# Splitting the second mixer's weights into DRAM during the first MLP

## The chip, the cores and the metric

The kernel runs on one core of a Trainium2 chip. The metric is device time in microseconds, the median of several runs. A core has five engines that matter here: TensorE (PE) for matmuls, VectorE (DVE) and ScalarE (ACT) for everything by element, GpSimd (POOL, almost unused) and SyncE (SP), which only issues DMAs. Each engine executes its own instructions in order. ACT can issue DMAs too.

## The reference

A trunk of two layers, 512 tokens with 16 meta tokens put ahead of them (528 positions), width 1024, fp32. Each layer is a mixer and an MLP, each between two RMS norms:

```
a = rmsnorm(h, mix_pre_g[l])
proj = a @ w_in[l]                      # q, k, v, b_gate, c_gate, hc
y_attn = sliding_window_gqa_sinks(q, k, v, sinks[l])   # q, k with partial rope
y_conv = short_gated_conv(b_gate, c_gate, hc, conv_w[l])
y = concatenate([rmsnorm(y_attn, attn_out_g[l]), rmsnorm(y_conv, conv_out_g[l])])
h = h + rmsnorm(y @ w_out[l], mix_post_g[l])
a = rmsnorm(h, mlp_pre_g[l])
f = square(relu(a @ w_up[l])) @ w_down[l]
h = h + rmsnorm(f, mlp_post_g[l])
```

`w_in` is 1024 x 2304, `w_out` 1024 x 1024, `w_up` 1024 x 4096, `w_down` 4096 x 1024, for each layer.

## The kernel before

Everything is kept transposed: channels on the 128 partitions, 8 blocks of them, and the 528 positions along the free axis. For accuracy each fp32 operand is split into a high part, rounded to the matmul's fp32r format, and a low part, the rest. A product of one block is three matmuls (`mm3`, L196 to L198): high by high, high by low, low by high.

Weights come in tiles of 1024 x 128. The list `blocks` names them in the order of use: for each mixer 2 tiles for k and v, 4 for q, 12 for the convolution's three inputs ("in") and 8 of the output projection ("out"); then the MLP in four chunks of 1024 hidden channels. Chunk 0 has 8 plain "up" tiles and 8 "down" tiles. Chunks 1 to 3 have 28 units of "upx" each, which are the seven products of Strassen's scheme for four pairs of tiles (`fast_pair`), and then 8 down tiles.

`prep()` (L134) makes a tile ready. SP loads its two halves of 256 KB each to `wraw` (5 buffers), and `cast()` splits each half: ACT copies it to the high part (L107), and DVE subtracts that from the raw half, which gives the low part (L108). High and low parts lie in 14 slots "w". After each tile used, `tile_done()` and `refill()` prepare further ones, so that up to 14 units are ready or under way. For two layers that is 264 splits of plain halves, and others for the pairs.

`mlp()` runs the chunks. `one()` multiplies one tile with both ranges of positions (A and B; in layer 0 two products of 24 matmuls) and evacuates each product from its PSUM bank: an up tile by `f_evac` (DVE's max, ACT's square, then a split into f_hi and f_lo), a down tile by `z_evac` (ACT copies for chunk 0, DVE adds for the others). In chunk 3 `one()` runs the first two down tiles only; the other six go to `boundary()`, where the last products in range B overlap with the norm of the first range and the next mixer's first products. There `Post` makes the norm's factor s (`chain`, L248 and L249), then for each block of channels the product with z (L326), the new h (L327), and a_hi and a_lo. `first_tiles` multiplies the mixer's k, v and first q tiles. After k and q are evacuated, the rope exchanges rows by small DMAs on SP (L558, L559), which stand in SP's order among the loads of weights.

The order of each engine's instructions is set by a scheduler, which simulates the program in time and places each instruction where it expects it to be ready. So an instruction written at one place can stand later on its engine, and from then on the order is fixed. All DMAs of weights are issued by SP in the kernel before; ACT issues a few at the start and two at the end.

Of the kernel before, what the change touches and what calls it, by code (L numbers as in the profile page):

```python
# [8 lines left out]
F32 = mybir.dt.float32  # L9
F32R = mybir.dt.float32r  # L10
AF = mybir.ActivationFunctionType
ALU = mybir.AluOpType

P = 128
# [22 lines left out]
def trunk_kernel(ctx, tc, xT, gains, sinkb, sinkm, rope, masks, maskm, ident_in, w_in, w_out, w_up, w_down, outT):  # L37
    nc = tc.nc
    ACT, DVE, POOL, PE = nc.scalar, nc.vector, nc.gpsimd, nc.tensor
# [3 lines left out]
    cp = ctx.enter_context(tc.tile_pool(name="cp", bufs=1))  # L43
# [7 lines left out]
    def tmp(w=272):  # L51
        return tp.tile([P, 272], F32, tag="t", name="t", bufs=8)[:, :w]
# [24 lines left out]

    epst = cp.tile([P, 4], F32, name="epst")

    blocks = []  # L80
    for l in range(2):
        blocks += [("in", l, 512), ("in", l, 640)]
# [13 lines left out]
    prepared = []  # L96
    last_load = []
# [5 lines left out]
    def half():  # L103
        return wp.tile([P, 4, P], F32, tag="wraw", name="wraw", bufs=5)

    def cast(raw, hi, lo):
        ACT.activation(hi, raw, AF.Copy)  # L107
        DVE.tensor_tensor(lo, raw, hi.bitcast(F32), ALU.subtract)  # L108
# [4 lines left out]
    def prep_pair(l, m, n):  # L113
# [17 lines left out]
        cast(pair[("A11", "S2", "S3", "S1", "A12", "A22", "S4")[n]], f[:, 0:4, :], f[:, 4:8, :])  # L131
        prepared.append((f[:, 0:4, :], f[:, 4:8, :]))

    def prep(beside=None):  # L134

        if len(prepared) == len(blocks):
            return
        taken[0] += size(len(prepared))
        kind, l, sub = blocks[len(prepared)]
        if kind == "upx":  # L140
            return prep_pair(l, *sub)
        hi = wp.tile([P, KT, P], F32R, tag="w", name="whi", bufs=2 * CAP)
        lo = wp.tile([P, KT, P], F32R, tag="w", name="wlo", bufs=2 * CAP)
        raws = []
        for i in range(2):
            raw = half()
            raws.append(raw)
            ks = slice(4 * i, 4 * i + 4)
            dma = nc.sync.dma_start
            if kind == "out":  # L150
                col = slice(P * sub, P * sub + P)
                if i == 0:
                    for g in range(2):
                        dma(raw[g * 64:(g + 1) * 64], w_out[l, g * 256:(g + 1) * 256, col].rearrange("(j p) m -> p j m", p=64))
                else:
                    dma(raw, w_out[l, 512:1024, col].rearrange("(k p) m -> p k m", p=P))
            elif kind == "q":
                for g in range(2):
                    last_load[:] = [dma(raw[:, :, 64 * g:64 * g + 64], w_in[l].rearrange("(k p) m -> p k m", p=P)[
                        :, ks, 256 * g + 64 * sub:256 * g + 64 * sub + 64])]  # L160
            elif kind == "down":
                c, m = sub
                dma(raw, w_down[l, c * 1024:(c + 1) * 1024, P * m:P * m + P].rearrange("(k p) m -> p k m", p=P)[:, ks, :])
            else:
                src, off = (w_in, sub) if kind == "in" else (w_up, P * sub)
                last_load[:] = [dma(raw, src[l].rearrange("(k p) m -> p k m", p=P)[:, ks, off:off + P])]
            if beside:

                beside[2 * i]()
                cast(raw, hi[:, ks, :], lo[:, ks, :])  # L170
                beside[2 * i + 1]()
        if not beside:
            for i in range(2):
                ks = slice(4 * i, 4 * i + 4)
                cast(raws[i], hi[:, ks, :], lo[:, ks, :])
        prepared.append((hi, lo))
# [8 lines left out]
    def refill(most=9):  # L185
        while len(prepared) < len(blocks) and taken[0] + size(len(prepared)) <= 2 * cap[0] and most:
            prep()
            most -= 1

    def tile_done(most=9):  # L190
        taken[0] -= size(done[0])
        done[0] += 1
        refill(most)
# [23 lines left out]
    def gemm(item, act):  # L217
        for ev in mms([item], act):
            ev()
# [31 lines left out]
    def utile():  # L251
        return tp.tile([P, L + 2], F32, tag="u", name="u", bufs=2)
# [2 lines left out]
        return tp.tile([P, 272], F32, tag="s", name="s", bufs=2)[:, :n]  # L255

    pend = []

    def flush():
        while pend:  # L260
            pend.pop(0)()
# [239 lines left out]
    def z_evac(m, r, add, final, col):  # L501

        t0, t1 = r
        l, c = col
        g = gt[:, l, c + m:c + m + 1]

        def ev(ps):
            zz = z[:, m, t0:t1]
            if add:
                DVE.tensor_tensor(zz, zz, ps, ALU.add)  # L510
                if final and l == 1 and m == 7 and r == RB:
                    sq = tmp(t1 - t0)
                    ACT.activation(sq, zz, AF.Square)
                    last_sq.append(sq)
                elif final:
                    add_sq("z", m == 0, zz, r)
                if final:
                    if l == 1:
                        ACT.activation(zz, zz, AF.Copy, scale=g)
            elif final:  # L520
                ACT.activation(zz, ps, AF.Copy, scale=g)
                add_sq("z", m == 0, ps, r)
            else:
                ACT.activation(zz, ps, AF.Copy)
        return ev

    class Mixer:
# [367 lines left out]
    def f_evac(m, r):  # L895
        t0, t1 = r

        def ev(ps):
            f = tmp(t1 - t0) if t1 - t0 <= 272 else utile()[:, :t1 - t0]
            DVE.tensor_scalar(f, ps, 0.0, None, ALU.max)  # L900
            ACT.activation(f, f, AF.Square)
            split(f_hi[:, m, t0:t1], f_lo[:, m, t0:t1], f)
        return ev

# [79 lines left out]
    def mlp(l, nxt, first):  # L984

        xr = xrange(l)

        full = xr if l == 0 else [(xr[0][0], xr[1][1])]

        def one(evac, act):  # L990
            w = wtile()
            for r in full:
                gemm((w, r, evac(r)), act)
            tile_done()

        txs[l] = [wp.tile([P, 4, L // 2], F32R, tag="x", name="tx", bufs=3) for _ in range(3)]
        for c in range(NCH):
            if c == 0:
                for m in range(NA, 8):
                    one(lambda r: f_evac(m, r), act_a)  # L1000
            else:
                for m in range(0, 8, 2):
                    fast_pair(l, m)
            last = c == NCH - 1
            if last:
                new_acc("h")
            for m in range(2 if last else 8):
                one(lambda r: z_evac(m, r, c > 0, last, (l, G_MPOST)), act_f)
                if c == 0 and m < 4:
                    fast_sums(l, m)  # L1010
        if nxt is not None:
            clear_pad()
        w = wtiles(6)
        for m in range(6):
            gemm((w[m], xr[0], z_evac(2 + m, xr[0], True, True, (l, G_MPOST))), act_f)
        boundary(l, w, act_f, G_MPOST, lambda r: Post(l, G_MPOST, r, nxt), first)
# [87 lines left out]
```

## Time and profile before

| | |
|---|---|
| median of 3 runs | 1096.59 us (1096.15 to 1097.74) |
| profiled execution | 1097.51 us |
| span in its profile | 1095.7 us |
| TensorE busy | 1074.3 us, 98% |
| DVE busy | 801.3 us, 73% |
| ACT busy | 624.6 us, 57% |
| DMA | mean 93 GB/s, 102.06 MB |

The first mixer ends and the first MLP's products begin near 180 to 230 us; chunk 0's down tiles run until 295 us, then pairs and down tiles alternate until 562 us; the second mixer runs until about 700 us, the second MLP to the end. In rows of groups of instructions the columns are: line, engine, operation, what is written from what, count, then busy time and mean duration, then idle time just ahead of them and what ended most of it.

### The profile page before, as it was taken

Reading aid. Unit: us, or ns where it says so; the run is one execution under the profiler, and the core shown is the slowest. Engines: PE = TensorE matmul, PEld = TensorE weight load, DVE = VectorE, ACT = ScalarE, POOL = GpSimd, SP = SyncE. Lnnn points to the kernel's source line nnn. Section 1 sums busy time; section 2 is a strip of 40 time slices with the busy share of each in tenths; the row PEclk is TensorE's granted clock in tenths of the full one; section 3 lists DMA queues with packets and bytes.
Section 4 is the critical chain, followed back from the end, with each engine's and each line's share of the span. In section 5 each row is a group of like instructions: output and inputs, shape, how many; then the busy total and the mean of one; then the engine's idle time right before and its main releaser. Section 6 shows DMA issues by size and latency. Waiting matters only on the chain.

```text
span 1095.7 us, 21642 instructions
## 1 busy us (share of the span) xinstructions
PE 1074.3 (98%) x8196; PEld 1030.8 (94%) x8196; DVE 801.3 (73%) x1895; ACT 624.6 (57%) x1510; POOL 10.8 (1%) x44
## 2 busy tenths in 40 slices
PE   8999999999999999999999999999999999999995
PEld 8999999999999999999989999999889989989995
DVE  7797886977585586586597988779947757757735
ACT  7576766665472383275365676667636625725732
POOL 2000000000000000000000000000000000000000
PEclk9999999999999999999999999999999999999998
DMA  9252122252252243144141412232422522522402
GB/s 249 64 146 59 58 78 79 77 155 59 69 152 85 59 127 110 49 124 137 26 112 39 130 58 59 78 97 82 130 72 84 154 68 79 162 68 71 143 1 77
DMA packets 206057, 102.06 MB, mean 93 GB/s; under 512 B 24000, under 2 KB 205904, under 8 KB 205952
## 3 DMA queue, kind: packets, MB, share of 16 engines
q1 hardware_dynamic: 205088, 99.89, 31.9%
q8 instruction: 64, 1.05, 0.4%
q10 hardware_dynamic: 688, 0.58, 0.2%
q14 instruction: 41, 0.34, 0.1%
q0 software_dynamic: 176, 0.21, 0.1%
HBM read 97.88 MB, written 2.10 MB: 91 GB/s over the span
## 4 chain that ended last, share of the span: by engine, by line
PE 88%; DVE 7%; ACT 1%; DMA 1%; issue 1%; SPq 1%; DVEq 0%; ACTq 0%
PE ps L196 28%; PE ps L198 28%; PE ps L197 28%; PE ps L202 1%; PE ps L684 1%; PE ps L653 1%; DVE wlo L108 1%; DVE a_lo L338 1%; DVE h L327 1%; DVE acc L280 1%; PE ps L235 1%; DMA h<-in_xT 0%; DVE t L326 0%; DMA z<-t 0%; SPq L558 0%
## 5 line engine op out<-in xcount | busy, mean ns | idle before, releaser
L197 PE MATMUL ps<-f_lo,whi 128*128 128x256 f32 (+2 forms) x1072 | 326.1, 305 | 0.0
L198 PE MATMUL ps<-f_hi,wlo 128*128 128x256 f32 (+2 forms) x1072 | 325.5, 305 | 0.0
L196 PE MATMUL ps<-f_hi,whi 128*128 128x256 f32 (+2 forms) x1072 | 322.9, 306 | 0.0
L197 PE MATMUL ps<-a_lo,whi 128*128 128x256 f32 (+3 forms) x808 | 230.2, 289 | 2.0 <-DVE a_lo L338 1.7
L196 PE MATMUL ps<-a_hi,whi 128*128 128x256 f32 (+3 forms) x808 | 227.2, 294 | 4.8 <-ACT a_hi L380 1.9
L198 PE MATMUL ps<-a_hi,wlo 128*128 128x256 f32 (+3 forms) x808 | 229.2, 288 | 0.1
L108 DVE TENSOR_TENSOR wlo<-wraw,whi 128x512 fp32r<-128x512 f32 x264 | 174.2, 688 | 51.8 <-ACT whi L107 31.5
L198 PEld LDWEIGHTS ps<-f_hi,wlo 128*128 128x128 f32 x1072 | 202.1, 189 | 9.1
L197 PEld LDWEIGHTS ps<-f_lo,whi 128*128 128x128 f32 x1072 | 201.6, 188 | 9.5
L107 ACT ACTIVATE whi<-wraw 128x512 fp32r<-128x512 f32 x264 | 153.9, 624 | 95.4 <-PE ps L197 58.4
L196 PEld LDWEIGHTS ps<-f_hi,whi 128*128 128x128 f32 x1072 | 199.5, 188 | 9.4
L196 PEld LDWEIGHTS ps<-a_hi,whi 128*128 128x128 f32 x808 | 148.1, 189 | 9.9 <-ACT a_hi L380 2.3
L197 PEld LDWEIGHTS ps<-a_lo,whi 128*128 128x128 f32 x808 | 152.6, 189 | 5.0 <-DVE a_lo L338 2.6
L198 PEld LDWEIGHTS ps<-a_hi,wlo 128*128 128x128 f32 x808 | 152.9, 189 | 1.4 <-DVE wlo L108 0.3
L510 DVE TENSOR_TENSOR z<-z,ps 128x272 f32<-128x272 f32 (+2 forms) x78 | 38.0, 487 | 99.9 <-PE ps L198 99.8
L107 ACT ACTIVATE wf<-wraw 128x512 fp32r<-128x512 f32 x96 | 59.7, 626 | 85.4 <-PE ps L197 51.8
L197 PE MATMUL ps<-a_lo,wf 128*128 128x264 f32 (+1 forms) x384 | 108.0, 282 | 0.0
L196 PE MATMUL ps<-a_hi,wf 128*128 128x264 f32 (+1 forms) x384 | 107.8, 282 | 0.0
L198 PE MATMUL ps<-a_hi,wf 128*128 128x264 f32 (+1 forms) x384 | 107.1, 283 | 0.0
L107 ACT ACTIVATE wf<-u 128x512 fp32r<-128x512 f32 x72 | 45.1, 627 | 88.4 <-PE ps L197 73.6
L108 DVE TENSOR_TENSOR wf<-wraw,wf 128x512 fp32r<-128x512 f32 x96 | 65.7, 688 | 11.5 <-ACT wf L107 10.5
L197 PEld LDWEIGHTS ps<-a_lo,wf 128*128 128x128 f32 x384 | 72.2, 188 | 0.1
(158 smaller groups left out, 1776.5 us busy)
## 6 DMA issues: line engine op xcount, KB each, us to landing
wraw<-in_w_up SPq DMA_DIRECT2D x128, 256.0 KB
wraw<-in_w_down SPq DMA_DIRECT2D x128, 256.0 KB
wraw<-in_w_in SPq DMA_DIRECT2D x56, 256.0 KB
wraw<-in_w_in SPq DMA_DIRECT2D x32, 128.0 KB
wraw<-in_w_out SPq DMA_DIRECT2D x32, 128.0 KB
wraw<-in_w_out SPq DMA_DIRECT2D x16, 256.0 KB
h<-in_xT SPq DMA_DIRECT2D x4, 272.0 KB
h<-in_xT SPq DMA_DIRECT2D x4, 256.0 KB
```

The lines of the kernel that those rows point to most:

```text
L107: ACT.activation(hi, raw, AF.Copy)
L108: DVE.tensor_tensor(lo, raw, hi.bitcast(F32), ALU.subtract)
L196: PE.matmul(ps, whi, ahi, start=first, stop=False, skip_group_check=onto)
L197: PE.matmul(ps, whi, alo, start=False, stop=False, skip_group_check=onto)
L198: PE.matmul(ps, wlo, ahi, start=False, stop=last, skip_group_check=onto)
L202: PE.matmul(ps, a[n], b[n], start=first and n == 0, stop=last and n == 1)
L235: PE.matmul(ps, ones[:, which, :], acc, start=True, stop=more is None)
L280: return (eng or DVE).tensor_tensor(acc, acc, sq, ALU.add)
L327: DVE.tensor_tensor(hk, hk, t, ALU.add)
L338: DVE.scalar_tensor_tensor(a_lo[:, k, t0:t1], hk, g, a_hi[:, k, t0:t1].bitcast(F32), ALU.mult, ALU.subtract)
L510: DVE.tensor_tensor(zz, zz, ps, ALU.add)
L653: PE.matmul(outs[g], q[a][rows], k[b][rows], start=n == 0, stop=n == 2)
```

## The change

Two buffers are added in SBUF: `sr` for a raw half of a tile, `sf` for its high and low parts. A new function `stash()` is called behind each product of `one()` in layer 0, and its instructions are queued behind that product's evacuation (`issue_after`). Each call takes one half of one of the second mixer's 26 tiles: it splits the half in `sr` into `sf` (ACT and DVE), ACT issues a store of `sf` (512 KB) to a tile in DRAM, and ACT issues the load of the next half into `sr`. The first call only loads. There are 58 calls and 52 halves, so the last calls do nothing. When `prep()` comes to such a tile, SP loads its four pieces (256 KB each) from DRAM straight into two slots "w", and nothing is split there. The matmuls are the same. The lines of `prep()` that loaded a half are moved to `load_half()`, for both uses.

```
+    sr = cp.tile([P, 4, P], F32, name="sr")
+    sf = cp.tile([P, 2, 4, P], F32R, name="sf")
+    dp = ctx.enter_context(tc.tile_pool(name="dp", bufs=1, space=bass.MemoryType.DRAM))
...
+    def load_half(queue, raw, kind, l, sub, i):
+        ks = slice(4 * i, 4 * i + 4)
+        dma = queue.dma_start
+        if kind == "out":
+            col = slice(P * sub, P * sub + P)
+            if i == 0:
+                for g in range(2):
+                    dma(raw[g * 64:(g + 1) * 64], w_out[l, g * 256:(g + 1) * 256, col].rearrange("(j p) m -> p j m", p=64))
+            else:
+                dma(raw, w_out[l, 512:1024, col].rearrange("(k p) m -> p k m", p=P))
+        elif kind == "q":
+            for g in range(2):
+                last_load[:] = [dma(raw[:, :, 64 * g:64 * g + 64], w_in[l].rearrange("(k p) m -> p k m", p=P)[
+                    :, ks, 256 * g + 64 * sub:256 * g + 64 * sub + 64])]
...
+    stashed = {}
+    to_stash = [(b, i) for b in blocks if b[1] == 1 and b[0] in ("in", "q", "out") for i in range(2)]
+
+    def stash():
+
+        if not to_stash:
+            return
+        if not stashed:
+            stashed[None] = None
+            return stash_load()
+        (kind, l, sub), i = to_stash.pop(0)
+        cast(sr, sf[:, 0], sf[:, 1])
+        t = dp.tile([P, 2, 4, P], F32R, name=f"st_{kind}_{sub}_{i}")
+        ACT.dma_start(t.bitcast(F32), sf.bitcast(F32))
+        stashed.setdefault((kind, l, sub), []).append(t)
+        stash_load()
+
+    def stash_load():
+        if to_stash:
+            block, i = to_stash[0]
+            load_half(ACT, sr, *block, i)
...
+        if (kind, l, sub) in stashed:
+            src = stashed[(kind, l, sub)]
+            for n, t in enumerate((hi, lo)):
+                for i in range(2):
+                    nc.sync.dma_start(t[:, 4 * i:4 * i + 4, :].bitcast(F32), src[i][:, n].bitcast(F32))
+            prepared.append((hi, lo))
+            return
...
+                last_ev[:] = [DVE.tensor_tensor(zz, zz, ps, ALU.add)]
...
+                last_ev[:] = [ACT.activation(zz, ps, AF.Copy)]
...
+            last_ev[:] = [ACT.activation(f, f, AF.Square)]
...
                 gemm((w, r, evac(r)), act)
+                if l == 0:
+                    with tc.issue_after(last_ev[0].ins):
+                        stash()
```

Lines shift by the added ones: the cast's two instructions are L113 and L114 in the changed kernel, the stash's store L174, its loads of "in" L159, the reloads L197.

DVE where the stash begins, in chunk 0 of the first MLP, in the changed kernel (wlo, wraw and whi belong to the usual splits, f_lo to an up tile):

```order
L940 TENSOR_SCALAR t_3433<-ps_3408 128x256
L114 TENSOR_TENSOR wlo_3444<-wraw_3445,whi_3443 128x512
L114 TENSOR_TENSOR wlo_3444<-wraw_3447,whi_3443 128x512
L114 TENSOR_TENSOR sf_88<-sr_87,sf_88 128x512
L324 TENSOR_TENSOR f_lo_73<-t_3433,f_hi_72 128x256
```

The first step's subtraction stands behind the two of a weight tile that were there before.

DVE at the layer boundary before (s is the norm's factor, L326 and L327 are the first steps of Post):

```order
L108 TENSOR_TENSOR wlo_7585<-wraw_7586,whi_7584 128x512
L108 TENSOR_TENSOR wlo_7585<-wraw_7588,whi_7584 128x512
L248 SCALAR_TENSOR_TENSOR t_7647<-ps_7643,t_7647 128x256
L249 SCALAR_TENSOR_TENSOR s_7642<-t_7647,t_7646 128x256
L326 SCALAR_TENSOR_TENSOR t_7680<-z_69,gt_76,s_7642 128x256
L326 SCALAR_TENSOR_TENSOR t_7685<-z_69,gt_76,s_7642 128x256
L327 TENSOR_TENSOR h_68<-h_68,t_7680 128x256
```

and at the same place now:

```order
L320 TENSOR_TENSOR acc_7247<-acc_7247,t_7792 128x272
L320 TENSOR_TENSOR acc_3080<-acc_3080,t_7829 128x256
L287 SCALAR_TENSOR_TENSOR t_7891<-ps_7887,t_7891 128x256
L288 SCALAR_TENSOR_TENSOR s_7886<-t_7891,t_7890 128x256
L114 TENSOR_TENSOR sf_88<-sr_87,sf_88 128x512
L366 SCALAR_TENSOR_TENSOR t_7924<-z_69,gt_76,s_7886 128x256
L366 SCALAR_TENSOR_TENSOR t_7929<-z_69,gt_76,s_7886 128x256
```

The two splits ahead of the norm are gone, and the subtraction of the 52nd step stands between s and the first product of Post.

ACT in the pairs of chunk 1, in the changed kernel (wf are the pairs' split weights, t and f_hi belong to the evacuation of products):

```order
L113 ACTIVATE wf_4522<-wraw_4443 128x512
L113 ACTIVATE sf_88<-sr_87 128x512
L997 ACTIVATE t_4504<-t_4504 128x264
L113 ACTIVATE wf_4542<-wraw_4441 128x512
L1013 ACTIVATE t_4525<-t_4525 128x264
L998 ACTIVATE t_4504<-t_4504 128x264
L323 ACTIVATE f_hi_72<-t_4525 128x264
L323 ACTIVATE f_hi_72<-t_4504 128x264
L113 ACTIVATE wf_4563<-u_4464 128x512
L174 DMA st_q_3_1_3924<-sf_88 128x1024
L159 DMA sr_87<-in_w_in 128x4x128
L997 ACTIVATE t_4545<-t_4545 128x264
```

Three instructions of a step, the cast, the store and the next load, now stand among those that evacuate the pairs' products, though no call of `stash()` is written there.

SP among the rope's exchanges of the second mixer, before:

```order
L558 DMA z_69<-t_7845 8x256
L559 DMA z_69<-t_7845 8x256
L166 DMA wraw_8075<-in_w_in 128x4x128
L166 DMA wraw_8164<-in_w_in 128x4x128
L166 DMA wraw_8166<-in_w_in 128x4x128
L558 DMA z_69<-t_7957 8x256
L559 DMA z_69<-t_7957 8x256
```

and in the changed kernel:

```order
L599 DMA z_69<-t_8246 8x256
L197 DMA whi_8264<-st_in_1792_0_4118 128x512
L197 DMA whi_8264<-st_in_1792_1_4160 128x512
L197 DMA wlo_8265<-st_in_1792_0_4118 128x512
L197 DMA wlo_8265<-st_in_1792_1_4160 128x512
L598 DMA z_69<-t_8295 8x256
L599 DMA z_69<-t_8295 8x256
```

Both have 40 exchanges there. Three loads of weights stood among them, now twelve reloads do.

More of the change, by code (lines that the diff above doesn't have):

```diff
@@ L132, in prep_pair @@
         prepared.append((f[:, 0:4, :], f[:, 4:8, :]))
+    def load_half(queue, raw, kind, l, sub, i):
[12 more added lines that the diff above has]
+                    :, ks, 256 * g + 64 * sub:256 * g + 64 * sub + 64])]
+        elif kind == "down":
+            c, m = sub
+            dma(raw, w_down[l, c * 1024:(c + 1) * 1024, P * m:P * m + P].rearrange("(k p) m -> p k m", p=P)[:, ks, :])
+        else:
+            src, off = (w_in, sub) if kind == "in" else (w_up, P * sub)
+            last_load[:] = [dma(raw, src[l].rearrange("(k p) m -> p k m", p=P)[:, ks, off:off + P])]
+    stashed = {}
[16 more added lines that the diff above has]
+            load_half(ACT, sr, *block, i)
     def prep(beside=None):
@@ L148, in prep @@
             ks = slice(4 * i, 4 * i + 4)
[L149 to L166, printed above, removed]
+            load_half(nc.sync, raw, kind, l, sub, i)
             if beside:
@@ L257, in trunk_kernel @@
     pend = []
+    last_ev = []
     def flush():
@@ L509, in ev @@
             if add:
-                DVE.tensor_tensor(zz, zz, ps, ALU.add)
+                last_ev[:] = [DVE.tensor_tensor(zz, zz, ps, ALU.add)]
                 if final and l == 1 and m == 7 and r == RB:
@@ L523, in ev @@
             else:
-                ACT.activation(zz, ps, AF.Copy)
+                last_ev[:] = [ACT.activation(zz, ps, AF.Copy)]
         return ev
@@ L900, in ev @@
             DVE.tensor_scalar(f, ps, 0.0, None, ALU.max)
-            ACT.activation(f, f, AF.Square)
+            last_ev[:] = [ACT.activation(f, f, AF.Square)]
             split(f_hi[:, m, t0:t1], f_lo[:, m, t0:t1], f)
```

## The prediction

> **What bounds the kernel now.** I read the page's first part, then the waits of the matmul engine, then busy time by stage, then the chain.
>
> ```profile
> span 1095.7 us, 21642 instructions
> PE 1074.3 (98%) x8196; PEld 1030.8 (94%) x8196; DVE 801.3 (73%) x1895; ACT 624.6 (57%) x1510; POOL 10.8 (1%) x44
> q1 hardware_dynamic: 205088, 99.89, 31.9%
> L108 DVE TENSOR_TENSOR wlo<-wraw,whi 128x512 fp32r<-128x512 f32 x264 | 174.2, 688 | 51.8 <-ACT whi L107 31.5
> L107 ACT ACTIVATE whi<-wraw 128x512 fp32r<-128x512 f32 x264 | 153.9, 624 | 95.4 <-PE ps L197 58.4
> ```
>
> TensorE is busy 1074.3 of 1095.7 us, so every edit outside it can win 21.4 us at most. The change leaves its matmuls alone. One split costs ACT 0.62 us (L107) and DVE 0.69 us (L108). All loads together hold the DMA engines 31.9% of the span.
>
> What the change could win lies in the second mixer, which begins near 562 us. The waits of TensorE between 540 and 640 us (total, count, mean) are:
>
> ```profile
> PE ps L196 <- DVE vv L284: 1.5, 1, 1.5
> PE ps L196 <- ACT acc L301: 1.3, 1, 1.3
> PE ps L202 <- ACT p L283: 1.2, 1, 1.2
> PE ps L235 <- DVE acc L280: 1.0, 1, 1.0
> PE ps L684 <- DVE S L638: 0.3, 1, 0.3
> ```
>
> Their sum is 5.3 us. Busy time by stage (the stretch, its length, then PE, PEld, DVE, ACT, POOL, granted clock, DMA share, GB/s) shows the three stages of pairs of the first MLP (chunks 1 to 3), the two down stages between them, the stage behind the third, and the part around the layer boundary:
>
> ```profile
> 295.00:335.00 40.00, 40.00 (x332) 40.00 (x331) 31.98 (x68) 30.24 (x71) 0.00 (x0) 1.00 0.48 139
> 335.00:382.00 47.00, 47.00 (x389) 47.00 (x388) 27.06 (x49) 11.96 (x22) 0.00 (x0) 1.00 0.22 62
> 382.00:423.00 41.00, 41.00 (x339) 41.00 (x338) 32.88 (x68) 30.57 (x72) 0.00 (x0) 1.00 0.46 136
> 423.00:470.00 47.00, 47.00 (x389) 47.00 (x388) 27.01 (x50) 12.36 (x22) 0.00 (x0) 1.00 0.22 63
> 470.00:510.00 40.00, 40.00 (x331) 40.00 (x330) 31.36 (x66) 30.15 (x70) 1.43 (x4) 1.00 0.47 139
> 510.00:558.00 48.00, 48.00 (x394) 47.92 (x393) 31.05 (x73) 18.99 (x44) 0.98 (x3) 1.00 0.27 64
> 540.00:632.00 92.00, 86.70 (x707) 82.83 (x705) 80.39 (x236) 55.95 (x150) 2.38 (x10) 1.00 0.32 88
> ```
>
> In the MLP TensorE never stops (40.00 of 40.00, 47.00 of 47.00): there is nothing to gain there and everything to lose. ACT has 35 us free in a down stage of 47, but under 10 in a stage of pairs of 40. From 540 to 632 us DVE is the full one (80.39 of 92).
>
> **The gain.** In the stretch 540 to 632 us the splits are:
>
> ```profile
> L108 DVE TENSOR_TENSOR wlo<-wraw,whi 128x512 fp32r<-128x512 f32 x26 | 17.0, 688 | 2.5 <-ACT whi L107 2.5
> L107 ACT ACTIVATE whi<-wraw 128x512 fp32r<-128x512 f32 x26 | 15.3, 626 | 6.7 <-DMA wraw<-in_w_in 6.6
> ```
>
> 17.0 us leave DVE and 15.3 ACT, beside PE waits of 5.3. Four of the five waits are on attention's and the norm's vector work, queued among these splits. The wait on acc L301 is a norm that runs through ACT and DVE alone near 562 to 579 us, with no split of a weight in it, so I leave its 1.3 out: gain 4.0, bounds 0 (the waits are chains that only become a little shorter) and 5.3 (all go).
>
> **The cost: one step.** 52 halves are split during the first MLP, one after another through one buffer for the raw half and one for the result. A step is a cast, a subtraction, the issue of a 512 KB store and the issue of the next load, and the next cast waits until both transfers have landed. Issues are priced by these rows (least, median, longest in ns):
>
> ```profile
> L118 SPq DMA_DIRECT2D wraw<-in_w_up x96: 367/368/1372, 237.2 to 1006.4; - x96
> L159 SPq DMA_DIRECT2D wraw<-in_w_in x32: 368/499/1736, 5.5 to 551.4; - x32
> L154 SPq DMA_DIRECT2D wraw<-in_w_out x32: 601/608/1214, 83.9 to 692.6; - x32
> L356 ACTq DMA_DIRECT2D outT<-h x2: 379/384/388, 1090.0 to 1092.4; - x2
> ```
>
> ACT's two stores at the end show that an issue costs ACT as much as SP. The stash's loads are 28 plain ones of "in" (0.37), 16 of "q" (0.50), 16 of the first halves of "out" (0.61) and 8 of its second halves (0.37): 10.4 + 8.0 + 9.7 + 3.0 = 31.1 us, 0.60 a step. So a step occupies ACT for 0.63 + 0.38 + 0.60 = 1.61 us, 84 us in all, and DVE for 0.69.
>
> Where the steps fall is read from the order. The first subtraction stands behind the pair of weights' subtractions at 230 us, the last one between the norm's factor s and the first product of Post, at 564 us in the times of before:
>
> ```profile
> 229.53 0.42 DVE L900 TENSOR_SCALAR t<-ps 128x256 f32<-128x256 f32 x1 [0.51 <-PE ps L198]
> 230.08 1.29 DVE L108 TENSOR_TENSOR wlo<-wraw,whi 128x512 fp32r<-128x512 f32 x2
> 563.99 0.42 DVE L249 SCALAR_TENSOR_TENSOR s<-t 128x256 f32<-128x256 f32 x1
> ```
>
> 51 steps thus have 564.4 - 231.4 = 333 us, a slot of 6.53 us each. By the order some 8 lie in each down stage (5.8 us apart) and 6 to 7 in each stage of pairs (6.4 apart), although no evacuation that they were queued behind is there: they run late, back to back.
>
> **How long is the round of a step?** Nothing like it runs before, so I bound it. A 256 KB load landing behind nothing is on the chain:
>
> ```profile
> 608.65 3.28 DMA wraw<-in_w_in
> 611.95 0.64 ACT whi L107
> 612.61 0.69 DVE wlo L108
> ```
>
> Least: 0.63 + 0.69 + 0.38 + 3.28 = 4.98 us, if the store costs nothing beside the load. Most: the store's bytes go ahead on the same queue. q1 moved 99.89 MB in 0.319 x 1095.7 = 349.5 us, 286 GB/s, so 0.524 MB add 1.83, and the transfers share the engines with SP's loads (share 0.22 to 0.48 of some 2.75 us: 0.6 to 1.3): 7.4 to 8.1 us. I take the middle of 4.98 and 8.1, 6.5, since the bytes must go through but the landing of store and load overlap.
>
> With a round of 6.5 against 5.8 in the order, ACT, which executes in order, ends a down stage 8.1 x 0.7 = 5.7 us late. That costs nothing by itself: the down stage needs from ACT only the next weights, 14 units of which are ready. But in the stage of pairs ACT has 30.2 us of its own plus 6.5 x 1.61 = 10.5, which is 40.7 of 40: it can't catch up. At the end of the stage stands the cover:
>
> ```profile
> 332.63 0.43 DVE L284 TENSOR_TENSOR f_lo<-t,f_hi 128x264 fp32r<-128x264 f32 x1 [0.71 <-ACT f_hi L283]
> 335.22 0.65 PE L196 MATMUL ps<-f_hi,whi 128*128 128x272 f32 x4
> ```
>
> The last piece of f is ready at 333.06 and used at 335.2, so 2.2 us of lateness are hidden. 5.7 - 2.2 = 3.5 us of wait, in three stages: 10.5 us. Bounds: 0 (the lateness is made up in ACT's idle stretches) and 3 x (5.7 + 0.7) = 19, with no cover. DVE, at 32 of 40 with 4.5 more, stays under its limit. The last step's subtraction on the chain at the boundary is 0.69 us, within the error of the rest.
>
> Sum against the profiled execution (1097.51): 1097.51 + 10.5 - 4.0 = 1104.0. The median of the runs, 1096.59, is 0.9 below it: **1103 us**.
>
> **Rivals.**
>
> *A, faster: the round fits.* If it is 5.8 us or less, ACT isn't late, and its 40.7 of 40 costs 0.7, under the cover of 2.2. Then only the gain is left: 1096.6 - 4.0 = 1092.6. For it: the least of 4.98, and DMA engines over half idle in every stage. Against it: the store's 1.83 alone takes the round past 5.8. The Trainium skill ("DMA: Bandwidth & Descriptors", "Anatomy of one DMA") has 2.0 us plus bytes at 436 GB/s; by that the load would be 2.6, an estimate, where the row has 3.28, so the row decides.
>
> *B, level.* A little of the lateness shows, 1 to 2 us in each stage, about as much as the mixer gains: 1096 to 1099.
>
> *C, much slower: the round is longer than even the mean slot.* At 7.2 us, 51 x (7.2 - 6.53) = 34 us too many for the whole MLP; less the cover 2.2 and the gain 4.0, about 1124. It decides from 6.53 us up, each 0.1 us costing 5. For it: the upper bound of 8.1, and "q" loads of narrow rows. Against it: stores and loads may overlap. The Trainium skill says in the same section that a completion "can cause a surprisingly long delay especially when the write target is HBM", which is the store's case; no trace of before has such a store ahead of its own buffer's reuse, and the round would be nearer 8 than 5 by it.
>
> *D, lost in the second mixer.* There SP has three loads among the rope's 40 little swaps before, and twelve after; a swap behind four reloads waits 4 x 0.45 = 1.8 us (0.45 lies between the issues of 0.37 and 0.50 above). The swaps and the loads among them stand close together:
>
> ```profile
> 578.94 0.71 SPq L558 DMA_DIRECT2D z<-t  x1
> 589.97 1.54 SPq L166 DMA_DIRECT2D wraw<-in_w_in  x3
> 607.98 0.62 SPq L559 DMA_DIRECT2D z<-t  x1
> 608.65 2.64 SPq L166 DMA_DIRECT2D wraw<-in_w_in  x5
> ```
>
> Nine more loads are 9 x 0.45 = 4 us on SP. If all of it reaches the attention, the gain is gone and A becomes 1096.6. Against it: a swap is used only after several further matmuls.
>
> That the change doesn't do what it says is excluded by the order: 52 halves are stored, and 104 reloads take the place of the splits.
>
> **Numbers.** Forecast 0.35, A 0.34, C 0.17, B 0.09, D 0.05. From 1091 (A with nearly the whole 5.3) to 1122 (C with a round just past the slot): what is left out is most of C and a little of A, under 2 in 10. The forecast's own range, with a loss of 6 to 15, is 1099 to 1108. A measurement of this kernel can tell 0.2%, 2.2 us, from no change. Faster by more: A and a little of B, 0.35. Within it: B, D and the edges, 0.12. Slower: 0.53.
>
> **What would show it.** A round of 6.5: consecutive stash casts 6 to 7 us apart in the down stages, idle time of ACT ahead of them released by the stash's own transfers. Lateness: TensorE waits on f_lo or f_hi at the start of each down stage of chunks 1 to 3, 3 to 4 us each, and none in the down stages. The gain: the waits on vv, p and acc L280 near 570 to 625 us gone. The forecast is wrong if casts come under 5.8 us apart (A), if waits come all through the MLP (C), or if the attention waits for z (D).

## The result and the profile after

The changed kernel takes 1124.56 us (median of 4 runs, 1122.27 to 1125.47), against 1096.37 for the kernel before on the same chip: 1.0248 times as long, 95% interval 1.0231 to 1.0264. The prediction had the side right (slower), the size wrong: 1103, with 1122 as the upper end.

The page after, first part and queues (q10 is ACT's queue), answers to the first fence of the prediction:

```profile
span 1123.5 us, 21903 instructions
PE 1086.5 (97%) x8196; PEld 1038.5 (92%) x8196; DVE 800.9 (71%) x1895; ACT 623.1 (55%) x1510; POOL 10.7 (1%) x44
q1 hardware_dynamic: 188256, 113.52, 34.4%
q10 hardware_dynamic: 39984, 41.48, 12.1%
```

DVE and ACT are busy as long as before: the splits were only moved. TensorE has the same 8196 matmuls but is 12.2 us longer busy with them, and the span is 27.8 us longer. Both halves of that difference have to be explained: waits of TensorE, and slower matmuls.

Where the time went is seen by comparing when TensorE's 2000th matmul starts (251.6 us before, in chunk 0's down tiles), its 4200th (519.3, past the last stage of pairs), its 4600th (570.1, past the layer boundary) and its 6200th (767.6, in the second MLP). The differences between the two traces, in us:

| stretch | changed kernel against before |
|---|---|
| up to the first step | -1.8 |
| the MLP's stages of pairs and down stages | +11.0 |
| the layer boundary | +13.3 |
| the second mixer | +5.0 |
| the second MLP | 0.0 |

Inside the MLP all of it lies in the stages of pairs and at their ends; from the 2800th to the 3000th matmul, for instance, and from the 3600th to the 3800th, both between down tiles, the traces do not drift apart at all. The 1.8 us at the start come and go between kernels (the first loads) and belong to no part of the change.

The waits of TensorE after, first between 285 and 590 us, then from 590 to 800 us (total, count, longest):

```profile
PE ps L235 <- ACT a_hi L373: 4.0, 2, 2.0
PE ps L235 <- ACT t L1003: 3.7, 5, 1.5
PE ps L274 <- DVE acc L320: 3.5, 1, 3.5
PE ps L235 <- DVE t L993: 2.4, 3, 1.1
PE ps L236 <- DVE f_lo L324: 1.0, 1, 1.0
PE ps L235 <- ACT f_hi L323: 0.9, 1, 0.9
PE ps L236 <- DVE a_lo L378: 0.5, 1, 0.5
...
PE ps L241 <- ACT p L323: 3.5, 1, 3.5
PE ps L235 <- ACT acc L341: 1.3, 1, 1.3
PE ps L235 <- DVE vv L324: 1.3, 1, 1.3
...
```

Before there was no wait at all from 220 to 540 us. The pairs' own evacuations (L1003, L993) cost 6.1 us, f_lo and f_hi at the ends of the stages only 1.9. That is 8.0 of the 11.0; the granted clock stays at 1.00 there, and at each of these waits the start of the next matmul moved some 0.2 to 0.4 us more than the wait itself, which makes up the rest. At the boundary it is the norm's sum (acc, 3.5), a_hi (4.0) and a_lo (0.5), 8.0 where 1.0 was before. In the second mixer the wait on p grew from 1.2 to 3.5, and the one on vv is still there.

What ACT waited for, in the steps' casts:

```profile
ACT sf L113 <- DMA sr<-in_w_in: 50.0, 32, 5.8
ACT sf L113 <- DMA sr<-in_w_out: 27.8, 13, 4.6
```

45 of the 52 casts wait for the load of their half, 77.8 us in all. Some of these loads on the chain of waits (start, length), two in a down stage and two in stages of pairs, and then the chain at the boundary, without its pieces of under 0.4 us:

```profile
357.10 4.10 DMA sr<-in_w_in
363.05 3.48 DMA sr<-in_w_in
...
309.76 6.76 DMA sr<-in_w_in
414.22 4.96 DMA sr<-in_w_in
...
538.93 4.67 DMA sr<-in_w_out
543.68 0.64 ACT sf L113
544.35 0.69 DVE sf L114
545.07 3.22 DMA st_out<-sf
548.31 5.57 DMA wlo<-st_in
553.88 0.69 DVE sf L114
554.60 5.44 DMA st_out<-sf
560.10 3.31 DMA wlo<-st_q
563.44 8.30 DMA sr<-in_w_out
571.75 4.97 DMA wlo<-st_q
```

From 538.9 to 577 us TensorE does not appear on this chain: load, cast, subtraction, store and reload take turns. A load that lands in 3.5 us among the down tiles takes 8.3 there.

And busy time in short stretches (length, PE, PEld, DVE, ACT, POOL, granted clock, DMA share, GB/s), three at a lowered clock and one between them for comparison:

```profile
549.82:553.23 3.41, 3.41 (x19) 3.41 (x18) 0.00 (x0) 0.02 (x1) 0.00 (x0) 0.50 1.05 227
573.71:583.95 10.24, 7.89 (x34) 7.60 (x35) 5.65 (x15) 3.14 (x8) 0.33 (x1) 0.50 0.76 276
648.80:652.22 3.42, 3.42 (x22) 3.20 (x19) 3.35 (x13) 1.45 (x5) 0.10 (x1) 0.50 1.00 362
555.00:560.00 5.00, 5.00 (x45) 5.00 (x44) 3.05 (x8) 2.08 (x5) 0.00 (x0) 1.00 0.79 258
```

Here are the slower matmuls: behind the wait of 3.5 us, which ends at 549.1, the granted clock is 0.50 for 3.41 us, and behind the first of the two waits on a_hi, which ends at 572.9, it is 0.50 for 10.24 us. By these rows some 5 us of the boundary's 13.3 are clock: 53 matmuls in 11.3 busy us, which at 45 in 5 us would take 5.9. Another 7.0 are the longer waits, 8.0 in place of 1.0. The third stretch lies behind the wait on p in the second mixer. The Trainium skill ("TensorE: Matmul & The Clock Gate", "Part 1: The HAM clock gate") says that the array falls to half its clock after about one idle window of 3.4 us and needs as long busy to come back. The first wait and the one on p agree with that, with 3.5 us idle and 3.4 at half clock. The second place differs: there a wait of 1.97 us, followed by one of 0.5, was enough.

### The profile page after: what moved, and what is told of

Read it like the earlier page. It is cut to its first block, busy times and chain, and to the rows that moved or that the text cites. A ratio compares the mean times of both kernels' runs of the same rounds, so it can differ in the third digit from the quotient of the medians.

```text
span 1123.5 us, 21903 instructions
## 1 busy us (share of the span) xinstructions
PE 1086.5 (97%) x8196; PEld 1038.5 (92%) x8196; DVE 800.9 (71%) x1895; ACT 623.1 (55%) x1510; POOL 10.7 (1%) x44
## 4 chain that ended last, share of the span: by engine, by line
PE 69%; DMA 15%; DVE 7%; ACT 5%; issue 2%; SPq 1%; ACTq 0%; DVEq 0%
PE ps L235 22%; PE ps L236 21%; PE ps L237 21%; DMA sr<-in_w_in 6%; DMA sr<-in_w_out 3%; PE ps L241 2%; PE ps L693 1%; PE ps L724 1%; DMA wraw<-in_w_up 1%; ACT sf L113 1%; DVE sf L114 1%; DMA z<-t 1%; ACT whi L113 1%; DVE a_lo L378 1%; DMA st_out<-sf 1%
## 5 line engine op out<-in xcount | busy, mean ns | idle before, releaser
L235 PEld LDWEIGHTS ps<-f_hi,whi 128*128 128x128 f32 x1072 | 200.6, 188 | 10.5 <-ACT f_hi L323 1.1
L114 DVE TENSOR_TENSOR wlo<-wraw,whi 128x512 fp32r<-128x512 f32 x212 | 140.1, 689 | 40.5 <-ACT whi L113 24.2
L113 ACT ACTIVATE whi<-wraw 128x512 fp32r<-128x512 f32 x212 | 123.5, 622 | 64.7 <-PE ps L236 38.0
L113 ACT ACTIVATE wf<-wraw 128x512 fp32r<-128x512 f32 x96 | 59.3, 623 | 55.5 <-PE ps L236 29.9
L113 ACT ACTIVATE wf<-u 128x512 fp32r<-128x512 f32 x72 | 45.0, 625 | 63.3 <-PE ps L236 48.1
L235 PEld LDWEIGHTS ps<-a_hi,wf 128*128 128x128 f32 x384 | 71.9, 188 | 6.7 <-ACT t L1003 4.7
L113 ACT ACTIVATE sf<-sr 128x512 fp32r<-128x512 f32 x52 | 32.8, 631 | 80.1 <-DMA sr<-in_w_in 50.0
```

The costliest lines, as they stand in the source:

```text
L235: PE.matmul(ps, whi, ahi, start=first, stop=False, skip_group_check=onto)
```

## The experiments

All are compared with the kernel before on their own chip. The last three columns are differences from the trace before, as in the table above; the start and the second MLP are left out.

| kernel | median us | ratio, 95% interval | MLP | boundary | mixer 2 |
|---|---|---|---|---|---|
| changed kernel | 1124.56 | 1.0248 (1.0231 to 1.0264) | +11.0 | +13.3 | +5.0 |
| steps only | 1118.09 | 1.0197 (1.0176 to 1.0217) | +10.9 | +9.3 | -0.6 |
| reloads only | 1098.14 | 1.0017 (1.0008 to 1.0027) | 0 | -1.6 | +3.0 |
| reloads of half the bytes | 1093.83 | 0.9977 (0.9966 to 0.9988) | 0 | -1.6 | -2.1 |
| without "out" | 1107.39 | 1.0095 (1.007 to 1.012) | +10.4 | -1.6 | +3.3 |
| small transfers, steps only | 1103.83 | 1.0073 (1.0059 to 1.0088) | +7.7 | 0 | -0.9 |
| two raw buffers | 1105.42 | 1.0081 (1.0058 to 1.0103) | +4.1 | -1.6 | +5.0 |
| reloads only, by GpSimd | 1099.48 | 1.0023 (1.0014 to 1.0032) | 0 | -1.6 | +3.3 |
| ten tiles, steps in down stages | 1101.93 | 1.0054 (1.0043 to 1.0066) | +0.6 | -1.6 | +5.8 |
| reloads only, two DMAs a tile | 1095.02 | 0.9987 (0.9978 to 0.9996) | 0 | -1.6 | -1.2 |
| tiles 1 to 5 and 12 to 16 | 1096.35 | 0.9997 (0.9988 to 1.0005) | +2.1 | -1.6 | -2.1 |
| first six tiles | 1095.10 | 0.9985 (0.9976 to 0.9993) | 0 | -1.6 | -0.4 |
| two raw buffers, two DMAs | 1112.48 | 1.014 (1.0127 to 1.0153) | +16.1 | -1.6 | -1.2 |
| the same, steps' DMAs by GpSimd | 1106.38 | 1.0102 (1.0079 to 1.0125) | +8.3 | +2.2 | -1.2 |
| ten tiles, two DMAs a tile | 1100.15 | 1.0026 (1.0015 to 1.0037) | +3.9 | -1.6 | +2.5 |
| tiles 1 to 5 and 12 to 16, no step before the pairs | 1093.07 | 0.997 (0.9958 to 0.9981) | 0 | -1.6 | -0.7 |

**The parts alone.** Steps only:

```
-        if (kind, l, sub) in stashed:
+        if False:
             src = stashed[(kind, l, sub)]
```

> All 52 steps run and are stored, but the second mixer's tiles are loaded and split as before, so no reloads. Theory: the loss of 27 us has three parts, 11 in the stages of pairs (the steps themselves), 13 at the layer boundary (last steps waiting behind the reloads' burst), 5 in the second mixer (reloads). Then only the first part is left here: about 1106 to 1109 us. Rival: the steps alone also make the boundary's 13 us, then about 1119 to 1121.

1118.09. My theory fell at one point: the steps alone make 9.3 of the boundary's 13.3, with no reload near. Its chain of waits there shows why:

```profile
539.30 3.57 DMA sr<-in_w_out
542.95 0.64 ACT sf L113
543.62 0.69 DVE sf L114
544.71 0.61 ACTq L147
545.65 3.01 DMA sr<-in_w_out
548.77 0.64 ACT sf L113
549.43 0.69 DVE sf L114
550.12 0.36 DVE acc L320
550.53 1.27 PE ps L274 x2
```

Round upon round of the stash, and behind the last one the sum that the norm's matmul (L274) waits for. The steps' order was fixed among the boundary's squares and sums, so a late step makes these late.

Reloads only, and reloads of half the bytes:

```
-    to_stash = [(b, i) for b in blocks if b[1] == 1 and b[0] in ("in", "q", "out") for i in range(2)]
+    to_stash = [(b, i) for b in [("in", 1, 512)] for i in range(2)]
...
-        if (kind, l, sub) in stashed:
-            src = stashed[(kind, l, sub)]
+        if l == 1 and kind in ("in", "q", "out"):
+            src = stashed[("in", 1, 512)]
```

```
-            for n, t in enumerate((hi, lo)):
+            for n, t in enumerate((hi,)):
...
-            prepared.append((hi, lo))
+            prepared.append((hi, hi))
```

> Only one tile (two steps) is split to DRAM, and all 26 tiles of the second mixer are reloaded from that one tile's two pieces, 1 MB each: this leaves out the other tiles' weights, so the second mixer computes with wrong weights, at the same cost in bytes and matmuls. Theory: no loss in the MLP, at the boundary little without late steps, the second mixer 5 us longer: about 1100 us (1098 to 1103). Rival 1, the prediction's gain: 1092.6. Rival 2, the burst of reloads alone makes the boundary's loss: 1108 or more.

> As the kernel that only reloads, but only the high parts are reloaded and used for the low parts too: it leaves out the low parts of the second mixer's weights, and 0.5 MB a tile are loaded, as many bytes as the raw weights before. Theory: without the doubled bytes the removed splits gain what was predicted, 1092 to 1094 us. Rival: bytes are not the cause, the time is that of the kernel that reloads both parts.

1098.14 and 1093.83, both in the theory's range. So the gain that the prediction priced at 4.0 exists: with no more loads than before, 1.6 are won at the boundary and 2.1 in the second mixer, 3.7 together. With both parts reloaded the mixer's 2.1 turn into a loss of 3.0, by TensorE's wait on p in the kernel with both (half the bytes are also half the reloads, two for a tile, so these two kernels don't tell bytes from issues):

```profile
PE ps L241 <- ACT p L323: 3.0, 1, 3.0
```

Without "out":

```
-    to_stash = [(b, i) for b in blocks if b[1] == 1 and b[0] in ("in", "q", "out") for i in range(2)]
+    to_stash = [(b, i) for b in blocks if b[1] == 1 and b[0] in ("in", "q") for i in range(2)]
```

> Only the 18 tiles of the input projection are split to DRAM (36 steps), the 8 of the output projection are loaded and split as before. The steps then end near 470 us, before the boundary, while the boundary's burst of reloads stays. Theory: the boundary's 13 us go except a few, the MLP's 11 shrink a little, the second mixer's 5 stay: about 1108 to 1112 us. Rival: the burst of reloads alone holds the boundary: 1119 to 1123.

1107.39, a little under what was expected. With the last step at 463 us nothing is lost at the boundary, reloads or not, and its gain of 1.6 appears. So the 13.3 need late steps; 9.3 come with the steps alone, and the 4 more only where steps and reloads meet.

**What in a step costs.** Small transfers: the raw half and the stored piece are cut to a quarter, with no reloads.

```
-        ACT.dma_start(t.bitcast(F32), sf.bitcast(F32))
...
+        ACT.dma_start(t.bitcast(F32), sf[:, :, 0, :].bitcast(F32))
...
-            load_half(ACT, sr, *block, i)
...
+            for g in range(2 if kind == "q" or kind == "out" and i == 0 else 1):
+                ACT.dma_start(sr[:, g, :], w_in[1, P * i:P * i + P, P * g:P * g + P])
```

> As the kernel of steps only (no reloads), but each transfer is cut to a quarter: a step loads one block of 64 KB in place of 256 KB and stores 128 KB in place of 512 KB (it leaves out the rest of the stored weights, which nothing reads). The number of casts, subtractions and DMA issues is the same. Theory of the round: ACT is late because it waits for landings; with shorter transfers the stages of pairs lose 4 us or less in place of 10.8 and the boundary 3 or less in place of 9.3: about 1099 to 1104. Rival, ACT's own work (casts and issues alone overfill the stages of pairs): no change from steps only, 1114 to 1119.

1103.83, at the upper end. The boundary's loss is gone; of the MLP's 10.9 there are 7.7 left, not 4. One wait of 4.3 us at the start of chunk 2's pairs, with 3.41 us at a granted clock of 0.50 behind it, makes 6.0 of them. But the edit changed more than the landings. A row of the store is now two pieces, and ACT's issues became dearer: a store's median is 0.53 us, where it is 0.35 in the kernel of steps only,

```profile
L175 ACTq DMA_DIRECT2D st_in<-sf x28: 526/527/591, 232.4 to 410.8; - x28
```

and all issues of the steps sum to 71.9 us in place of 57.0. So how much of the 7.7 is ACT's own time is not separated here.

Two raw buffers: the loads alternate between `sr` and the buffer `rt`, which is free then, and are issued a step ahead.

```
+    srs = [sr, rt[:, :512].rearrange("p (k m) -> p k m", k=4)]
...
-        stash_load()
+        stash_load(1)
...
-            load_half(ACT, sr, *block, i)
+            load_half(ACT, srs[(stashed[None] + n) % 2], *block, i)
```

> The whole change, with a second buffer for the raw half (the buffer of the rope's norm factors, which is free during the MLP), so a load is issued a step ahead and its landing is no longer in the round. Theory of the round: a round then is cast, subtraction and the store's landing, some 5 us, the stages of pairs lose 5 or less in place of 11, the last steps run before the boundary and its loss is halved: about 1108 to 1114. Rival (the store's landing or ACT's work sets the round): as the changed kernel, 1121 to 1126.

1105.42, better than expected: the same work, the same bytes and issues, and 11.0 become 4.1, 13.3 become -1.6. So 21.8 of the 24.3 us lost up to the mixer's start hang on one single buffer: the load could not be issued before the cast and the subtraction of the half before, so the steps ran late. Now the casts wait for the store (`st_in<-sf`), and the last step is done at 527 us.

**What in the reloads costs.** Reloads by GpSimd, and reloads by two DMAs of 512 KB for a tile:

```
-                    nc.sync.dma_start(t[:, 4 * i:4 * i + 4, :].bitcast(F32), src[i][:, n].bitcast(F32))
+                    POOL.dma_start(t[:, 4 * i:4 * i + 4, :].bitcast(F32), src[i][:, n].bitcast(F32))
```

```
-        ACT.dma_start(t.bitcast(F32), sf.bitcast(F32))
...
+        ACT.dma_start(t[:, :, 4 * i:4 * i + 4, :].bitcast(F32), sf.bitcast(F32))
...
-                for i in range(2):
-                    nc.sync.dma_start(t[:, 4 * i:4 * i + 4, :].bitcast(F32), src[i][:, n].bitcast(F32))
+                nc.sync.dma_start(t.bitcast(F32), src[:, n].bitcast(F32))
```

> As the kernel that only reloads (wrong weights in the second mixer, all from one tile), but the reloads are issued by GpSimd, on a queue of their own, in place of SP's queue. Theory: the 4 us that reloads cost in the second mixer come from the rope's small exchanges queued behind them on SP's queue; then they go: 1092.5 to 1094.5. Rival: the doubled bytes fill the DMA engines whichever queue they are in: 1097 to 1100 as with SP, or more if GpSimd issues them slowly.

> As the kernel that only reloads through SP (wrong weights in the second mixer, all from one tile), but the two halves of a stored tile lie together, so that SP issues two reloads of 512 KB for a tile and not four of 256 KB. By the order six issues stand among the rope's exchanges, not twelve; the bytes are the same. Theory: the 4 us that reloads cost in the second mixer are issue time on SP ahead of the exchanges; then most of it goes: 1093.5 to 1095.5. Rival: it is the bytes on the DMA engines: 1097 to 1099.

By GpSimd 1099.48: no gain, as the rival had it, but the wait moved. The one on p was gone, one on vv had grown from 1.4 to 4.0, since a swap of the rope landed only after 5.79 us, in which the DMA engines were busy for 0.98 of the time (the chain of waits of that kernel, start and length):

```profile
582.03 0.62 SPq L598
582.70 5.79 DMA z<-t
```

With SP and half as many issues the kernel takes 1095.02, as expected: the mixer gains 1.2 in place of losing 3.0, with the same bytes. Its last swap is issued at 607.5 us and not at 609.4; the swaps on its chain land in 1.79 us, as with four reloads a tile. So on SP's queue most of the loss was SP's time for issues, and it stays 0.9 short of the 2.1 that are gained with half the bytes. (A row of these reloads is also 4 KB long and not 2; no run separates that.) On a queue of their own the reloads' bytes can still hold the swaps up. Both occur, at different places.

**Putting mends together.** Ten tiles, with one step behind each of the first seven down tiles of chunks 0 to 2:

```
...
+                if l == 0 and not last and m < 7:
+                    with tc.issue_after(last_ev[0].ins):
+                        stash()
```

> The change cut to the first 10 tiles of the second mixer (20 steps), one step behind each of the first seven down tiles of chunks 0 to 2, so that by the order no step lies in a stage of pairs or near the boundary; the output is the reference's. Theory: steps in down stages cost nothing, the boundary gains the 1.6 us that the kernel of reloads gained there, the later tiles are loaded raw as before: 1094 to 1096. Rival: steps cost in the down stages too, or the reloads at the boundary delay the first products: 1097 or more.

> The first ten tiles, one step behind each of the first seven down tiles of chunks 0 to 2 (as the kernel of steps in down stages), but reloaded by two DMAs of 512 KB for a tile. Output as the reference. Theory: the wait of 5 us behind SP's exchanges shrinks to under 1: 1095 to 1097. Rival: it is where raw loads follow reloads, and stays: 1100 to 1102.

1101.93, and 1100.15 with two DMAs for a tile; 1094 to 1096 and 1095 to 1097 were expected. The steps cost next to nothing in the first (0.6), but the mixer loses 5.8: SP's last swap is issued at 611.1 us (608.0 before), raw loads follow only then, and the softmax waits on DVE behind their splits. In the second the mixer's loss is 2.5 and 3.9 are lost in the MLP. Neither expectation held; the second time is the rival's, but not for its reason alone, since the mixer's loss did shrink.

First six tiles only, and the first five with the twelfth to sixteenth, both with two DMAs:

```
+    to_stash = [(b, i) for b in [b for b in blocks if b[1] == 1][:6] for i in range(2)]
...
```

```
+    to_stash = [(b, i) for b in [b for b in blocks if b[1] == 1][:5] + [b for b in blocks if b[1] == 1][11:16] for i in range(2)]
...
```

> The same with the first 6 tiles only (k, v and q; 12 steps, in the down stages of chunks 0 and 1). Output as the reference. Theory: only the boundary's 1.6 is gained and nothing lost: 1094 to 1095.5. Rival: even these reloads, 6 MB at the boundary where 3 MB were, cost as much as they gain: 1096 to 1097.

> Ten tiles split to DRAM, one step behind each of the first seven down tiles of chunks 0 to 2, as in the kernel of steps in down stages; but the tiles are the first 5 (k, v and the first q) and the 12th to 16th, and a tile is reloaded by two DMAs. By the order no reload stands among the rope's exchanges, only the three raw loads that stood there before. Output as the reference. Theory: the boundary gains 1.6, the later tiles up to 2.3 in the attention, no wait is added: 1092 to 1094.5. Rival: reloads behind the exchanges still delay the attention's splits: 1096 or more.

1095.10, as expected, and 1096.35, where 1092 to 1094.5 were expected; it can't be told from before. In the second the mixer does gain 2.1, but the MLP loses 2.1 at the start of chunk 2's pairs. ACT's timeline of that kernel there:

```profile
380.60 0.37 ACT L1003 ACTIVATE t<-ps 128x264 f32<-128x264 f32 x1
382.36 0.63 ACT L113 ACTIVATE sf<-sr 128x512 fp32r<-128x512 f32 x1 [1.39 <-DMA sr<-in_w_in]
382.90 0.61 ACT L113 ACTIVATE wf<-u 128x512 fp32r<-128x512 f32 x1
```

The last step's cast waits for its load, and the pairs' weights (wf) stand behind it.

Both mends for the whole change, and then with the steps' stores and loads issued by GpSimd:

> The whole change, all 52 steps, with both mends: two raw buffers, and reloads by two DMAs of 512 KB for a tile. Theory: the kernel with two raw buffers, less the 4 us of SP's issues in the second mixer: 1100 to 1103, so a loss of 4 in the stages of pairs is what is left of the 27. Rival: the second mixer's wait stays: 1104 to 1107.

> The whole change, all 52 steps, with two raw buffers and reloads by two DMAs of 512 KB, and the steps' stores and loads issued by GpSimd in place of ACT, which then only makes the casts. Output as the reference. Theory: what the kernel with both mends lost in the stages of pairs, 16 us against 4 with the other layout of the store, was ACT's time for issues (about 0.3 us more per step); without any issue on ACT the loss there is under 2, the boundary and the second mixer gain 2.8: 1093 to 1096. Rival: it was the slower landing of the stores (pieces of 2 KB): 1106 or more, and GpSimd's issues may add to it.

1112.48 and 1106.38, where 1100 to 1103 and 1093 to 1096 were expected. The second mixer came out as meant in both (-1.2). The MLP did not: with the store in pieces of 2 KB it lost 16.1 in place of 4.1, though ACT's order in the MLP is the same. A store's issue takes ACT 0.52 us there and not 0.35:

```profile
L178 ACTq DMA_DIRECT2D st_in<-sf x28: 345/345/411, 233.6 to 434.0; - x28
```

```profile
L180 ACTq DMA_DIRECT2D st_in<-sf x28: 520/521/577, 233.0 to 442.8; - x28
```

(the first row is the kernel with two raw buffers, the second that with two DMAs as well; least, median, longest in ns). All issues of the steps sum to 60.4 and 79.2 us of ACT, 19 us more. With the issues on GpSimd the stages of chunks 2 and 3 lose 1.1 in place of 11.7, so there the issues' time on ACT is the likely cause. But chunk 1's stage loses 7.2 and the boundary 2.2: three casts of chunk 1's stage wait 8.5 us for stores there, one of them 4.2, where four waited 5.0 with the issues on ACT, and a store takes up to 8.9 us from its issue to its landing. That is the likely reason. The time is the rival's, 1106 or more, and the theory holds for two stages of three. A slower landing is hardly what made 16.1 out of 4.1: from 290 to 520 us ACT's casts wait 50.5 us for transfers in the kernel with both mends, and 50.9 in the one with two raw buffers.

Last, the kernel of five and five tiles with no step near a stage of pairs: a step behind each of chunk 0's three up tiles, and none behind the seventh down tile.

```
+                    one(lambda r: f_evac(m, r), act_a)
+                    if l == 0:
+                        with tc.issue_after(last_ev[0].ins):
+                            stash()
...
-                if l == 0 and not last and m < 7:
+                if l == 0 and not last and m < 6:
```

> As the kernel with the first 5 and the 12th to 16th tiles, but the 20 steps stand one behind each of chunk 0's three up tiles and the first six down tiles of chunks 0 to 2, so none behind the seventh down tile. Output as the reference. Theory: the 2.1 us lost at the start of chunk 2's stage of pairs came from the last step's cast, which waited for its load ahead of the pairs' weight splits on ACT; without it that loss is 0 and the gain of the boundary and the second mixer, about 3, is left: 1092.5 to 1094.5. Rival: the loss there is only moved to another place: 1095.5 or more.

1093.07, ratio 0.997 (0.9958 to 0.9981): 0.3% below the kernel before, within what can be had from the splits at all (3.7). The trace shows 2.3 us of it, at the boundary and in the mixer; the rest of its shorter span lies at the start. The MLP's loss is 0 with the same 20 steps. So these 20 steps between chunk 0's up tiles and between down tiles cost TensorE nothing, as none is near a stage of pairs. Its waits of TensorE:

```profile
PE ps L235 <- DVE vv L324: 2.0, 1, 2.0
PE ps L236 <- DVE a_lo L378: 1.7, 2, 0.9
PE ps L235 <- ACT acc L341: 1.3, 1, 1.3
PE ps L449 <- POOL ones L445: 1.0, 1, 1.0
PE ps L235 <- ACT a_hi L420: 0.9, 2, 0.7
PE ps L276 <- ACT t L553: 0.5, 1, 0.5
PE ps L236 <- DVE a_lo L424: 0.2, 1, 0.2
```

None is left in the MLP, and the wait on p, 1.2 before, is gone.

## Why the prediction was right or wrong

**Where the sum failed.** It had 10.5 in the stages of pairs, nothing at the boundary and -4.0 in the mixer, 6.5 in all. Measured were 11.0, 13.3 and 5.0, and -1.8 at the start. Two steps failed: the boundary, which was put at 0.69 us "within the error of the rest", and the gain, which turned into a loss. The stages of pairs came to the predicted size, in part by luck, as said below.

**The bound** was read rightly: nothing to gain in the MLP, a few us in the second mixer, TensorE's work unchanged. What it missed is that a wait of some us also lowers the clock afterwards: at the boundary the waits grew by 7.0, and 13.3 us were lost.

**The gain** of 4.0 was the right size for taking the splits away: 3.7 with half the bytes. What failed is the step that put 9 more loads on SP at 4 us into a rival of 0.05 only (D). In the kernel that only reloads the mixer was 3.0 longer in place of 2.1 shorter, which is 5.1; in the changed kernel it was 5.0 longer. The reason that I gave against it, that a swap is used only after several further matmuls, didn't hold for the last swaps: p, behind them, waited 3.5, and the clock was at 0.50 for 3.42 us after it.

**The round.** Taken as 6.5, the middle of 4.98 and 8.1. Measured as the mean distance of casts it is 6.98 (from 230.1 to 585.9 us, 51 rounds), 5.3 to 6.2 mostly in the down stages, 7.3 on average in the stages of pairs, 7.7 to 14 in the last four, at the boundary. One mean for all stages was the mistake: the load lands mostly in 3.5 to 4.2 us where DMA share is 0.65, and mostly in 4.1 to 6.8 where it is about 0.8, and the wait comes where ACT has no time for it. ACT's issues were priced too low as well: 50.9 us in the sum (31.1 for loads and 52 x 0.38 for stores), 59.0 measured. The estimate of 2.6 for a load, which the prediction set beside its row, goes by a fit that the Trainium skill ("DMA: Bandwidth & Descriptors", "Anatomy of one DMA") gives for DMAs that GpSimd issues; these loads are SP's and ACT's, and landed in 3.28 us and more.

**The stages of pairs**: 10.5 predicted, 11.0 measured, but by another way. I let ACT be late at the end of each down stage and show at f_lo; there it was hardly late, and 6.1 of the waits stand among the pairs' own evacuations and 1.9 at f. The two raw buffers (4.1) show that the wait for the load's landing is the larger part. The small transfers (7.7) fit less well, but their issues were dearer. The kernel with both mends (16.1) fits ACT's own time being the other part, since there any further us comes out at TensorE.

**The boundary** is the step that failed most. "The last step's subtraction on the chain at the boundary is 0.69 us" counted one instruction. But 8 steps stood behind the last pairs, each with a load to wait for, among the norm's squares and sums. It cost 13.3, of which 9.3 come with the steps alone and 4 more with the reloads, 1 MB for a tile where 0.5 MB were. That the bytes double stands nowhere in the sum; whether the reloads' bytes or their issues cost the 4 at the boundary no run separates.

**The rivals.** C came to the time (about 1124), with lateness of 51 times the round less the slot. That it met the number is luck. By its own sum the measured round of 6.98 gives some 17 more (51 x 0.45 = 23, less 2.2 and 4.0) and not 27.5; most of the rest is D, the mixer's 5.0 longer in place of 4.0 shorter. Nor do the 23 confirm it by lying near the 24.3 of MLP and boundary: the first and the last cast have fixed places in the order of their engine, so their mean distance holds the delay already. What confirms its mechanism, lateness of the steps through the round, is the kernel with two raw buffers, which takes the load out of the round and 21.8 out of the 24.3. A didn't occur, though its mechanism, a hidden step, is what the last kernel has. The forecast and C were one mechanism with two rounds, D another that adds to both: they were treated as if only one could be.

## What to carry to other kernels

Work moved into a stretch where the bottleneck never waits is only free if the engine that it moves to can wait there too: look stage by stage, since one buffer that chains load, work and store turns every landing into a wait of an in-order engine. Count the issues of DMAs as work of the engine that makes them, on both ends of a spill, and count its bytes twice where high and low parts come back. And a step that is late at a boundary costs more than its own length, through what is ordered behind it and through the clock.

## What the runs showed of the hardware

After a long wait of TensorE the granted clock was 0.50 for 3.41 us, or for two or three times that, and a matmul of 128x256 outputs took 0.40 to 0.43 us in place of 0.28. Between 220 and 1000 us of these traces every wait of 2.7 us or more was followed by that, and no wait up to 1.7 us was. Of those near 2 us only some were: one of 2.0 us in the last kernel was (0.50 from 588.4 to 591.8 us), one of 2.0 us in the kernel with two raw buffers was not (1.00 from 593.6 to 597 us). A DMA's issue on ACT took 0.35 us for a store of 4 KB rows and 0.52 where each row was two pieces of 2 KB, with the same bytes; in the same kernel the unchanged loads also rose, from 0.45 to 0.63 us. And while 4.85 MB went through SP's queue from 561 to 579 us, ACT's own issue took up to 1.28 us and its load 8.3 us to land.
